# The opening of an eight-unit RWKV-7 recurrence, issued in another order

## The chip, the cores and the metric

The kernel runs on one core of one Trainium2 chip. The metric is the device time of one execution in microseconds, as the median of several runs. Engines are named as the profile names them: PE (TensorE matmul; PEld is its weight load), DVE (VectorE), ACT (ScalarE), POOL (GpSimd), SP (SyncE, which here issues DMAs only).

## The reference

The model is a two-layer decoder trunk over 1040 tokens (16 meta tokens and 1024 drawn ones). Layer 0 mixes tokens by an RWKV-7 recurrence, layer 1 by stick-breaking attention, and each layer has a conv-gated MLP. Only the recurrence bears on the change:

```python
def rwkv7_time_mix(x, ...):
    ...
    seq = tuple(jnp.moveaxis(t, 1, 0) for t in (rh, decay, kh, vh, -kk, kk * ah))
    def step(S, inp):
        r_t, w_t, k_t, v_t, a_t, b_t = inp
        sa = jnp.einsum('bhij,bhj->bhi', S, a_t)
        S = (S * w_t[:, :, None, :] + sa[..., None] * b_t[:, :, None, :]
             + v_t[..., None] * k_t[:, :, None, :])
        return S, jnp.einsum('bhij,bhj->bhi', S, r_t)
    S0 = jnp.zeros((bsz, N_HEADS, HEAD_DIM, HEAD_DIM), f32)
    _, y = lax.scan(step, S0, seq)
    ...                                  # group norm of y, bonus, gate g, output weight w_o
```

There are 16 heads of width 64; the state of a head is 64 x 64.

## The kernel before

The projections of layer 0 (up to 593 us in the trace) leave their results in DRAM scratch: `AR_s`, `BK_s`, `vc_s`, `g_s`, `b_s`. Then `rwkv_chain` runs the recurrence, and after it come the output weight, the MLP and layer 1.

**Tiling.** The recurrence is done by chunks of 64 tokens. A unit is (q, s): four of the 16 heads (two pairs, index u) and one of two halves of the sequence, with eight chunks (NC = 8). There are eight units, (0,0), (1,0), (2,0), (3,0), (0,1) and so on. The first 16 tokens are a chunk of their own, `first_chunk`, for all heads together. It gives the state that the four units of s = 0 start from.

**A unit is prepared by generators.** Each `yield` is a place at which another generator may be run:

- `stage_a` loads `BK` and `ARz` (2 and 4 DMAs, 2 MiB together), multiplies them into the blocks `Aa` (PE, masked copies by DVE), stores the diagonal 16 x 16 blocks to scratch (`AD`, 8 DMAs) and loads them back with one block in each partition (`AT`).
- `stage_s` inverts those blocks by 30 small dependent instructions (`substitute`; tiles `prd` and `XL`), on DVE for unit (0,0) and on POOL for the rest, and stores the result (`XD`).
- `stage_x` loads it back (`Dz`, 8 DMAs), and doubles the inverses from 16 to 32 and to 64 by three rounds of small matmuls: `g` and `x` (with DVE's transpose `DT`, ACT's copies `Gz` and `X`), then `G` (`GT`), then `G` again, into `XTb`.
- `stage_b`, `stage_t`, `stage_v` make `Ar`, `BKt`, `UV` and `KV`. `stage_f` is the group norm of the outputs.

`first_chunk` does the same in small: loads (`fa`, `fb`), products `A0`, blocks to scratch `AD0` and back as `AT0` (in `fb`), `substitute` on POOL (in `fg`), inverse to scratch `XD0` and back as `XT0` (in `fb`), then `c20`, `c30`, the states, `yp0`, and its own group norm.

**The chain.** `stage_c` does a unit's eight chunks one after another: c1 (state by `ARz`), `Rz` (DVE), c2 (`Rz` by `XTb`; halves `c` and `c2b`), copies to `UV` (DVE and ACT), c3, new state (DVE), and outputs `yp`. Between these it calls `gap()`, which runs pieces of the next units' generators by the strings in `SEQ`.

**What sets the order.** Before unit (0,0)'s chain the list `PRE` (L1413) sets the order of generator steps: a letter names a generator (a, b, s, t, v, x of unit (0,0); A and S of unit (1,0); p is `stage_a` of unit (2,0); f is `first_chunk`; c clears tiles; W warms PE with matmuls of no use), a number says how many steps. What is left is run afterwards, and `first_chunk` at least until its four states are there. PE's matmuls and all instructions that go through the wrapper `InOrder` (L36: `LQ` is SP, `V` is DVE, `G` is POOL) keep the order in which the program issues them. ACT's copies do not: a scheduler places them by its own estimate of when they are ready. Every engine executes its queue in order.

SP's DMAs signal eight semaphores in turn. A DMA that comes to a semaphore waits until the DMA eight places ahead of it, which signalled the same one, has landed.

## Time and profile before

| what | us |
|---|---|
| median of 3 runs | 3543.39 (3541.86 to 3548.19) |
| the profiled execution | 3554.61, of which 3551.8 is the span from first to last instruction |
| opening of the recurrence, last projection store to first c1 | 594.58 to 690.65 |
| the recurrence's eight units | 690.65 to about 1104 |
| PE busy over the span | 3126.4 (88%), 27421 instructions |
| DVE, ACT, POOL busy | 2277.8 (64%), 1546.3 (44%), 1617.6 (46%) |
| mean granted TensorE clock over the span | 0.936 |

Read it by stages: the shares are means over stages with different limits. In the opening, where the change is, no engine is busy for long, and the time goes to waits of one queue for another.

### The profile page before, as it was taken

The numbers are of one execution on the slowest core, as the hardware profiler recorded it, in microseconds if no ns is written. First come the engines' busy times: TensorE is split into PE (matmuls) and PEld (weight loads), VectorE is DVE, ScalarE is ACT, GpSimd is POOL, SyncE is SP. The second block draws the span as 40 slices with busy tenths as digits, with TensorE's granted clock in tenths as the row PEclk, the third lists the DMA queues.
The fourth block names the chain that finished last, engine by engine and source line by source line (L and its number), as shares of the span: only waits on it lengthen the run. The fifth ranks groups of instructions, "written<-read, shape, count | busy, mean of one in ns | idle before, by whom it ended". The sixth has DMA issues, their size and how long they took to land.

```text
span 3551.8 us, 66931 instructions
## 1 busy us (share of the span) xinstructions
PE 3126.4 (88%) x27421; PEld 2946.2 (83%) x27421; DVE 2277.8 (64%) x3047; ACT 1546.3 (44%) x2849; POOL 1617.6 (46%) x1469
## 2 busy tenths in 40 slices
PE   6997886588889799999899888888889699998998
PEld 5896665577778699999899888888788699998998
DVE  7779675133334888887542577777764988887342
ACT  4654542244443333333332366666654333334232
POOL 5556444222325554544321566666544544454221
PEclk8998998699988899999999899999999799999999
DMA  6344434233335222222654100101036122224453
GB/s 210 117 157 152 131 127 139 62 81 87 100 92 167 84 74 76 73 78 72 197 167 122 48 25 25 31 25 27 19 123 193 66 79 78 79 72 145 126 170 93
DMA packets 436716, 354.22 MB, mean 100 GB/s; under 512 B 66919, under 2 KB 360573, under 8 KB 436155
## 3 DMA queue, kind: packets, MB, share of 16 engines
q1 hardware_dynamic: 433883, 343.39, 31.8%
q0 software_dynamic: 2528, 6.57, 0.5%
q8 instruction: 215, 3.52, 0.4%
q14 instruction: 90, 0.74, 0.1%
HBM read 255.96 MB, written 93.92 MB: 99 GB/s over the span
## 4 chain that ended last, share of the span: by engine, by line
PE 47%; DVE 16%; ACT 6%; DMA 4%; issue 4%; POOL 3%; SPq 1%; ACTq 0%; DVEq 0%; POOLq 0%
PE dn L1577 12%; DVE t L1760 5%; DVE om L2314 2%; PE kps L2159 2%; DVE rs L1685 2%; PE c L826 2%; PE A L826 2%; PE wt L2162 2%; PE av L2159 1%; ACT t L1758 1%; PE vps L2159 1%; PE wo L1969 1%; POOL be L2317 1%; PE sop L2159 1%; PE z L2159 1%
## 5 line engine op out<-in xcount | busy, mean ns | idle before, releaser
L1577 PE MATMUL dn<-act,h_dn 128*128 128x260 f32 x2688 | 437.9, 284 | 6.2 <-ACT act L76 3.1
L1577 PEld LDWEIGHTS dn<-act,h_dn 128*128 128x128 f32 x2688 | 373.5, 190 | 7.5 <-ACT act L76 3.5
L1760 DVE SCALAR_TENSOR_TENSOR t<-u,pcol,t 128x1040 f32<-128x1040 f32 x168 | 304.2, 1811 | 108.6 <-ACT t L1758 108.5
L1577 PE MATMUL dn<-act,l_dn 128*128 128x260 f32 x1344 | 273.5, 285 | 1.8 <-POOL l_dn L1526 1.7
L2317 POOL TENSOR_TENSOR be<-be,om 128x911 f32<-128x911 f32 (+7 forms) x128 | 195.7, 1529 | 131.9 <-DVE om L2314 105.6
L1526 POOL TENSOR_TENSOR l_dn<-r_dn,h_dn 128x1024 fp32r<-128x1024 f32 (+1 forms) x46 | 102.9, 2237 | 326.0 <-ACT h_dn L76 325.5
L2314 DVE TENSOR_TENSOR_SCAN om<-om 128x912 f32<-128x912 f32 (+7 forms) x128 | 213.8, 1670 | 50.2 <-POOL om L2309 30.5
L76 ACT ACTIVATE h_dn<-r_dn 128x1024 fp32r<-128x1024 f32 (+1 forms) x92 | 90.7, 985 | 297.8 <-PE dn L1577 287.2
L1775 POOL TENSOR_TENSOR t<-t,t 128x1040 f32<-128x1040 f32 x42 | 103.3, 2460 | 250.6 <-DVE t L1760 250.6
L1577 PEld LDWEIGHTS dn<-act,l_dn 128*128 128x128 f32 x1344 | 207.4, 189 | 2.2 <-POOL l_dn L1526 2.2
L1526 POOL TENSOR_TENSOR s34l<-rs,s34h 128x1024 fp32r<-128x1024 f32 x44 | 106.1, 2410 | 101.9 <-ACT s34h L76 101.9
L76 ACT ACTIVATE WT<-wt 128x512 fp32r<-128x512 f32 (+2 forms) x224 | 98.7, 443 | 121.3 <-PE wt L2162 92.5
L2380 DVE TENSOR_TENSOR WT<-wt,WT 128x512 fp32r<-128x512 f32 (+2 forms) x224 | 107.7, 489 | 54.2 <-ACT WT L76 53.4
L2159 PE MATMUL av<-WT,VS 128*128 128x256 f32 (+3 forms) x640 | 108.9, 284 | 33.5 <-DVE WT L2380 33.4
L76 ACT ACTIVATE s34h<-rs 128x1024 fp32r<-128x1024 f32 x44 | 46.7, 1062 | 200.4 <-PE p001S L1712 4.9
L1526 DVE TENSOR_TENSOR l_dn<-r_dn,h_dn 128x1024 fp32r<-128x1024 f32 (+1 forms) x46 | 52.1, 1132 | 121.7 <-ACT h_dn L76 121.6
L2162 PE MATMUL wt<-ident,be 128*128 128x128 f32 x576 | 100.4, 298 | 33.6 <-DVE WTm L2355 33.5
L2159 PEld LDWEIGHTS av<-WT,VS 128*64 128x64 f32 (+1 forms) x640 | 85.9, 166 | 44.8 <-DVE WT L2380 43.7
L2309 POOL TENSOR_SCALAR_AFFINE_SELECT be<-be 128x128 f32<-128x128 f32 x128 | 78.9, 617 | 94.9 <-ACT be L2304 94.7
L44 POOL TENSOR_TENSOR prd<-AT,XL 128x15 f32<-128x15 f32 (+7 forms) x105 | 28.2, 269 | 204.8 <-DMA AT<-AD 197.1
L826 PE MATMUL A<-ARz,BK 128*128 128x128 f32 x512 | 94.2, 328 | 30.3 <-DMA ARz<-AR_s 19.3
L2162 PEld LDWEIGHTS wt<-ident,be 128*128 128x128 f32 x576 | 80.1, 155 | 39.5 <-DVE WTm L2355 36.2
(2142 smaller groups left out, 11035.6 us busy)
## 6 DMA issues: line engine op xcount, KB each, us to landing
r_dn<-in_ffn_down_dram SPq DMA_DIRECT2D x60, 512.0 KB
a_s<-t SPq DMA_DIRECT2D x84, 260.0 KB
rv<-in_ffn_up_dram SPq DMA_DIRECT2D x42, 512.0 KB
ra<-in_ffn_up_dram SPq DMA_DIRECT2D x42, 512.0 KB
araw<-a_s SPq DMA_DIRECT2D x50, 260.0 KB
r_dn<-in_ffn_down_dram SPq DMA_DIRECT2D x32, 384.0 KB
raw<-a_s SPq DMA_DIRECT2D x36, 260.0 KB
hr<-h_s SPq DMA_DIRECT2D x32, 260.0 KB
```

The costliest lines, as they stand in the source:

```text
L76: return S.activation(o, i, AF.Copy, scale=scale)
L826: return tc.keep_in_program_order(mm(*args, **kw))
L1526: eng.tensor_tensor(lo, x, f(hi), op=ALU.subtract)
L1577: self.mm(ps[:, c, :], w[:, kk, :], X[k][i][:, c * CH : (c + 1) * CH], start=k == 0 and j == 0, stop=k == len(X) - 1 and j == 2,)
L1760: VV.scalar_tensor_tensor(t[j], u[j][:, i : i + n], w, t[j], op0=ALU.mult, op1=ALU.add)
L1775: (G if n == L else VV).tensor_tensor(t[1], t[0], t[1], op=ALU.mult)
L2159: return tc.keep_in_program_order(mm(*args, **kw))
L2162: return tc.keep_in_program_order(nc.tensor.transpose(*args))
L2309: G.affine_select(out=t[0:nq, 0:nq], in_=t[0:nq, 0:nq], compare_op=ALU.is_ge, fill=fill, base=-nq, pattern=[[1, nq]], channel_multiplier=1,)
L2314: V.tensor_tensor_scan(om[0:nq, 0:nk], om[0:nq, 0:nk], om[0:nq, 0:nk], 1.0, op0=ALU.mult, op1=ALU.min)
L2317: G.tensor_tensor(be[0:nq, 1:nk], be[0:nq, 1:nk], om[0:nq, 0 : nk - 1], op=ALU.mult)
L2380: V.tensor_tensor(wt[:, 1, s0:s1], ps[:, s0:s1], f(wt[:, 0, s0:s1]), op=ALU.subtract)
```

## The change

Seven edits, all in the opening or in pieces that the opening and the units share:

1. `first_chunk` issues its four small loads `vc0` together with its `fa` loads.
2. It gets one more yield between the stores `AD0` and the load `AT0`.
3. Its product `kv0` comes ahead of its `substitute`.
4. Its stores `XD0` and loads `XT0` go by POOL's queue (`G`) where SP's (`LQ`) issued them.
5. `stage_a` gets one more yield between `AD` and `AT` for units (0,0) and (1,0), and `stage_s` of unit (0,0) stores `XD` by SP where POOL did.
6. In `stage_x` ACT's copy of the diagonal blocks into `X` is written behind the products `g` and their copy, where it stood ahead of them.
7. `PRE` is another list, and `needs` asks for less.

```diff
@@ first_chunk
-            yield
             for q in range(4):
                 qs = slice(2 * q, 2 * q + 2)
                 LQ.dma_start(vc0[:, qs], vc_s[0][q][:, :, 0:16])
+            yield
...
             for e in range(2):
                 LQ.dma_start(AD0[e].rearrange("p j t -> j p t"), Aa0[32 * e : 32 * e + 16, :, e, 0:16])
+            yield
...
             yield
+            ps = ps_t("kv0")
+            for p in range(NP):
+                for e in range(2):
+                    vs = slice(32 - 32 * e, 64 - 32 * e)
+                    pmm(ps[32 * e : 32 * e + 32, p * 64 : p * 64 + 64], Aa0[vs, p, e, :], UV0[vs, p, e, :], start=True, stop=True)
+            copy_act(fg[0:64, 0:512], ps[0:64])
+            yield
             G.tensor_copy(XL0, xinit0)
             yield from substitute(XL0, AT0, pr0, 16, lambda j: G, 4)
             G.memset(XT0, 0.0)
             XD0 = dr.tile([2, NP, 16, 16], F32, name="XD0")
             xdv = XD0.rearrange("e p (i g) t -> g (e p) i t", g=4)
             for g in range(4):
-                LQ.dma_start(xdv[g], XL0[32 * g : 32 * g + 16])
+                G.dma_start(xdv[g], XL0[32 * g : 32 * g + 16])
             for e in range(2):
-                LQ.dma_start(XT0[32 * e : 32 * e + 16, :, 0:16], XD0[e].rearrange("p j t -> j p t"))
-            yield
-            ps = ps_t("kv0")
...
+                G.dma_start(XT0[32 * e : 32 * e + 16, :, 0:16], XD0[e].rearrange("p j t -> j p t"))
@@ stage_a
+            if s == 0 and q < 2:
+                yield
             AT = ed["AT"] = place(f"AT{q % 2}", f"AT{nm}")
@@ stage_s
-            G.dma_start(XD.rearrange("b u c i t -> (b u c) (i t)"), XL.rearrange("p i t -> p (i t)"))
+            (G if s + q else LQ).dma_start(XD.rearrange("b u c i t -> (b u c) (i t)"), XL.rearrange("p i t -> p (i t)"))
@@ stage_x
-            copy_act(Xv[:, :, 0:16], D[:, :, 0:16])
             ps = ps_t(f"g16{nm}")
...
             copy_act(Gl[:, :, 0:16], ps[:, 0:256].rearrange("p (m t) -> p m t", t=16))
+            copy_act(Xv[:, :, 0:16], D[:, :, 0:16])
@@ rwkv_chain
         PRE = (
-            "a2 W2 f c2 a11 s9 A2 s9 f s9 b9 s9 f v t5 b11 A12 x2 f4 x3 f8 v20 x3 S10 f8 x3 S10 f8 x3 S12 "
-            "f20 x21 p2 W3 f "
+            "a2 f c A2 v a8 a f a f b9 A8 A A f s t5 f v20 s30 s x c f30 f x4 W2 f x4 f x6 p2 S33 W f "
         ).split()
...
-        needs = {"s": "a", "S": "A", "v": "a", "b": "a", "t": "a", "x": "cs"}
+        needs = {"s": "a", "S": "A", "x": "s"}
```

Behind `first_chunk`'s states, what is left of it (its group norm and its eight stores `y_s`) is no longer run in `PRE`: it is pulled by the gaps of unit (0,0).

On SP's queue, before: the last `fa` load, unit (0,0)'s eight stores `AD`, the load `AT`, and then unit (1,0)'s loads. A row's bracket says what it waits for; DMAHW0 to DMAHW7 are the eight semaphores in turn, and DVE, Pool and Activation are those engines.

```order
L44 DMA fa<-BK_s_124 128x2x64 [waits DMAHW0_49]
L44 DMA AD_5804<-Aa_5803 16x16x16 [waits DMAHW1_49,DVE_49]
L44 DMA AD_5804<-Aa_5803 16x16x16 [waits DMAHW2_49]
L44 DMA AD_5804<-Aa_5803 16x16x16 [waits DMAHW3_49]
L44 DMA AD_5804<-Aa_5803 16x16x16 [waits DMAHW4_49]
L44 DMA AD_5804<-Aa_5803 16x16x16 [waits DMAHW5_49]
L44 DMA AD_5804<-Aa_5803 16x16x16 [waits DMAHW6_49]
L44 DMA AD_5804<-Aa_5803 16x16x16 [waits DMAHW7_49]
L44 DMA AD_5804<-Aa_5803 16x16x16 [waits DMAHW0_49]
L44 DMA AT_5837<-AD_5804 128x256 [waits DMAHW4_49,DMAHW3_49,DMAHW5_49,DMAHW2_49,DMAHW6_49,DMAHW1_49,DMAHW7_49,DMAHW0_49,Pool_49]
L44 DMA BK_10_5850<-BK_s_122 128x1024 [waits Activation_49]
L44 DMA BK_10_5851<-BK_s_122 128x1024
```

And now, from the last of eleven loads that stand ahead of `AD` (four `vc0`, two `BK`, four `ARz`, one `vc`):

```order
L44 DMA vc_5807<-vc_s_129 128x2x512 [waits DMAHW3_49]
L44 DMA AD_5810<-Aa_5809 16x16x16 [waits DMAHW4_49,DVE_49]
L44 DMA AD_5810<-Aa_5809 16x16x16 [waits DMAHW5_49]
L44 DMA AD_5810<-Aa_5809 16x16x16 [waits DMAHW6_49]
L44 DMA AD_5810<-Aa_5809 16x16x16 [waits DMAHW7_49]
L44 DMA AD_5810<-Aa_5809 16x16x16 [waits DMAHW0_49]
L44 DMA AD_5810<-Aa_5809 16x16x16 [waits DMAHW1_49]
L44 DMA AD_5810<-Aa_5809 16x16x16 [waits DMAHW2_49]
L44 DMA AD_5810<-Aa_5809 16x16x16 [waits DMAHW3_49]
L44 DMA AD_5865<-fa 16x8x16 [waits DMAHW4_49,DVE_49]
L44 DMA AD_5865<-fa 16x8x16 [waits DMAHW5_49,DVE_49]
L44 DMA AT_5868<-AD_5810 128x256 [waits DMAHW3_49,DMAHW6_49,DMAHW2_49,DMAHW7_49,DMAHW1_49,DMAHW0_49]
```

The loads of unit (1,0) moved ahead of the stores, so that the eighth store stands eight places behind the load `vc` and shares its semaphore, DMAHW3; `first_chunk`'s two stores (`AD_5865`) moved ahead of `AT`.

On PE before, from the products of the first doubling to `first_chunk`'s c20 (`c_6416`); `kv_6398` is its kv0:

```order
L826 MATMUL g_6055<-DT_6045,Aa_5803 32x16 x64
L829 MATMUL vt_6131<-ident,vc_5974 64x128 x4
L829 MATMUL vt_6138<-ident,vc_5974 64x128 x4
L829 MATMUL vt_6145<-ident,vc_5974 64x128 x4
L829 MATMUL vt_6152<-ident,vc_5974 64x128 x4
L826 MATMUL kv_6159<-UV_6129,Aa_5803 64x64 x16
L826 MATMUL kv_6177<-UV_6129,Aa_5803 64x64 x16
L826 MATMUL x_6195<-Dz,Gz 32x16 x64
L826 MATMUL G_6286<-X32T_6047,Aa_5803 32x32 x32
L826 MATMUL G_6340<-XTb_5733,GT_6319 32x32 x32
L826 MATMUL kv_6398<-UV_5938,fa 32x64 x16
L826 MATMUL c_6416<-fg,fb 32x64 x16
```

And now, up to the first c1 of the chain (`c_6499`); each matmul here is two records in the trace:

```order
L826 MATMUL kv_6062<-UV_6014,Aa_5809 64x64 x16
L826 MATMUL g_6166<-DT_6162,Aa_5809 32x16 x64
L826 MATMUL warm<-ident 128x128 x4
L826 MATMUL c_6239<-fg,fb 32x64 x16
L826 MATMUL c_6258<-UV_5933,BKt_5932 64x64 x16
L826 MATMUL x_6275<-Dz,Gz 32x16 x64
L826 MATMUL G_6346<-X32T_6164,Aa_5809 32x32 x16
L826 MATMUL yp_6371<-fa,UV_5933 64x16 x16
L826 MATMUL G_6346<-X32T_6164,Aa_5809 32x32 x16
L826 MATMUL G_6408<-XTb_5733,GT_6405 32x32 x32
L826 MATMUL warm<-ident 128x128 x2
L826 MATMUL c_6499<-S_6363,ARz_5735 64x64 x4
```

`first_chunk`'s c20 and c30 moved from behind unit (0,0)'s doubling into it: they now stand between its products g and x.

On ACT before, from the start of unit (0,0)'s state (`PS000`) on; `X3210` is unit (1,0)'s X, `c2b000` the first c2:

```order
L76 ACTIVATE PS000_6532<-S00_6452,PC_160 128x64 x2
L76 ACTIVATE fb_5783<-yp0_6460 128x128
L920 ACTIVATE ysq0_6486<-fb_5783 128x128
L938 ACTIVATE g20_6493<-g00_6491 128x2
L76 ACTIVATE ysq0_6486<-g10_6492 128x128
L76 ACTIVATE BKt10_6543<-bt1000_6544 128x512
L76 ACTIVATE X3210_6681<-Dz_5766 128x16x16
L76 ACTIVATE UV00_6129<-c2b000_6554 64x2x64
```

And now:

```order
L1216 ACTIVATE XTb0_5733<-X3200_6163 32x16x32 x4
L76 ACTIVATE PS000_6498<-S00_6363,PC_160 128x64 x2
L76 ACTIVATE X3210_6662<-Dz_5766 128x16x16
L76 ACTIVATE fb_5777<-yp0_6371 128x128
L920 ACTIVATE ysq0_6509<-fb_5777 128x128
L76 ACTIVATE GT00_6405<-G00_6346 32x512 x2
L76 ACTIVATE XTb0_5733<-G200_6408 32x16x32 x2
L76 ACTIVATE BKt10_6512<-bt1000_6513 128x512
L76 ACTIVATE UV00_6014<-c2b000_6523 64x2x64
```

Unit (1,0)'s copy X, which waits for unit (1,0)'s `Dz`, moved from just ahead of the first c2's copy to ahead of unit (0,0)'s last two doublings (`GT00`, `XTb0`).

## Rows read from the trace of the kernel before

**Rows 1.** Busy time by windows, opening: window, length, engines, clock, DMA share, GB/s

```profile
594.58:690.65 96.07, 49.66 (x776) 43.88 (x776) 22.10 (x67) 18.26 (x39) 32.47 (x93) 0.65 0.34 73
```

**Rows 2.** Chain that ended last, 580 to 760: start us, us, what

```profile
652.55 1.88 DMA Dz<-XD
...
675.67 1.93 PE c L826 x32
...
678.87 1.97 PE c L826 x32
...
686.94 1.24 PE warm L826 x4
...
693.28 6.61 DMA ARz<-AR_s
```

**Rows 3.** Timeline of SP's issues: start us, us, queue, line, out<-in, count

```profile
607.60 0.52 SPq L44 DMA_DIRECT2D fa<-BK_s  x1
611.63 3.79 SPq L44 DMA_DIRECT2D AD<-Aa  x8
616.71 0.34 SPq L44 DMA_DIRECT2D AT<-AD  x1
...
628.07 0.69 SPq L44 DMA_DIRECT2D fb<-AD  x1
...
649.19 3.81 SPq L44 DMA_DIRECT2D Dz<-XD  x8
667.13 2.57 SPq L44 DMA_DIRECT2D XD<-fg  x4
...
694.68 7.00 SPq L44 DMA_DIRECT2D Dz<-XD  x8
```

**Rows 4.** Timeline of POOL; in brackets its idle time and what ended it

```profile
632.55 0.62 POOL L44 DMA_DIRECT2D XD<-XL  x1 [21.08 <-DVE XL L44]
...
634.39 0.21 POOL L44 TENSOR_TENSOR fg<-fb,fg 128x15 f32<-128x15 f32 x1
```

**Rows 5.** Timelines of DVE, PE and ACT, in order of time for each

```profile
618.86 0.17 DVE L44 TENSOR_TENSOR prd<-AT,XL 128x15 f32<-128x15 f32 x1 [7.25 <-DMA AT<-AD]
...
655.31 1.90 PE L826 MATMUL g<-DT,Aa 32*32 32x16 f32 x128 [12.38 <-DVE DT L44]
...
666.61 0.17 PE L826 MATMUL x<-Dz,Gz 32*32 32x16 f32 x1 [2.37 <-issue]
...
698.85 1.19 PE L826 MATMUL A<-ARz,BK 128*128 128x128 f32 x4 [7.50 <-DMA ARz<-AR_s]
...
700.83 0.37 PE L826 MATMUL c<-Rz,XTb 128*64 128x64 f32 x1
...
670.16 1.20 ACT L76 ACTIVATE GT<-G 32x512 f32<-32x512 f32 x2 [0.28 <-PE G L826]
673.36 1.18 ACT L76 ACTIVATE XTb<-G 32x512 f32<-32x512 f32 x2 [2.00 <-PE G L826]
...
702.99 0.42 ACT L76 ACTIVATE X<-Dz 128x256 f32<-128x256 f32 x1 [1.47 <-DMA Dz<-XD]
```

**Rows 6.** Windows: two of full DMA load, then three of substitutions (DVE, POOL, POOL)

```profile
600.00:605.00 5.00, 0.10 (x1) 0.13 (x1) 0.00 (x0) 0.00 (x0) 4.85 (x4) 0.50 1.05 200
620.00:625.00 5.00, 1.26 (x6) 1.29 (x7) 4.52 (x20) 0.00 (x0) 0.00 (x0) 0.50 1.03 300
...
618.86:622.70 3.84, 0.00 (x0) 0.00 (x0) 3.31 (x16) 0.00 (x0) 0.00 (x0) 0.50 0.98 344
634.39:637.78 3.39, 2.68 (x15) 1.94 (x16) 0.00 (x0) 3.05 (x7) 2.53 (x12) 0.85 0.02 5
728.24:738.95 10.71, 10.16 (x241) 8.50 (x236) 3.97 (x14) 7.57 (x20) 8.18 (x30) 1.00 0.24 76
```

**Rows 7.** DMA issues, 630 to 745: count, KB each, median us to landing

```profile
XD<-XL POOLq DMA_DIRECT2D x3, 128.0 KB, 2.0
```

**Rows 8.** Tile stA on POOL: count, ns min/median/max of one

```profile
L1599 POOL TENSOR_TENSOR stA<-stA x24: 1287/1313/2300, 1114.3 to 2753.7; 128x520 f32<-128x520 f32 x24
```

More of the change, by code (lines that the diff above doesn't have):

```diff
@@ L1042, in first_chunk @@
             for g in range(4):
-                LQ.dma_start(xdv[g], XL0[32 * g : 32 * g + 16])
+                G.dma_start(xdv[g], XL0[32 * g : 32 * g + 16])
             for e in range(2):
-                LQ.dma_start(XT0[32 * e : 32 * e + 16, :, 0:16], XD0[e].rearrange("p j t -> j p t"))
-            yield
-            ps = ps_t("kv0")
-            for p in range(NP):
-                for e in range(2):
-                    vs = slice(32 - 32 * e, 64 - 32 * e)
-                    pmm(ps[32 * e : 32 * e + 32, p * 64 : p * 64 + 64], Aa0[vs, p, e, :], UV0[vs, p, e, :], start=True, stop=True)
-            copy_act(fg[0:64, 0:512], ps[0:64])
+                G.dma_start(XT0[32 * e : 32 * e + 16, :, 0:16], XD0[e].rearrange("p j t -> j p t"))
             yield
```

## Prediction, made before the changed kernel ran

> **What bounds the kernel now.** I read the windows first: the opening lasts 96.07 us, and in it PE is busy for 49.66, POOL for 32.47, DVE for 22.10, DMA for a third [rows 1]. No engine is the limit there, so what it costs is set by one queue waiting for another. The chain of waits and the queues say which. Unit (0,0)'s inverse is ready when POOL stores it at 632.55 [rows 4], and lands 2.0 us later [rows 7], but SP issues the loads `Dz` only at 649.19 [rows 3]: ahead of them on SP stand unit (1,0)'s stores `AD`, which wait for PE. That is 14 us of queue order. First_chunk's inverse starts at 634.39 [rows 4], is interleaved with unit (1,0)'s on POOL, and is stored only at 667.13 [rows 3]; c20 follows at 675.67, c30 at 678.87 [rows 2]. Last, unit (2,0)'s loads are issued behind first_chunk's output stores, so PE stands 7.50 us before A at 698.85, and c2 of the first chunk, which PE has behind A, starts at 700.83 [rows 2, 5]. From there the eight units run as a chain. I measure the change at that c2.
>
> **The change, part by part.**
>
> *Loads ahead of the stores (edits 1, 2, 5, 7).* The last `fa` load is issued at 607.60, taking 0.52 [rows 3]. Four `vc0` loads at 0.64 each (the pace of the four `XD` in 2.57, rows 3) end at 610.7. Then come 2.62 MB: `BK`, `ARz` and `vc`. By the ring of eight, the eighth store `AD` waits for `vc` to land. At 300 GB/s that is 8.7 us, at 200 it is 13.1, the two paces of full queues [rows 6]; with 2.0 for a landing [rows 7], 621.4 or 625.8. I take 621.4, since the 300 is from this same set of loads. Before, `AT` was issued 1.8 after the last of the eight stores (616.71 against 614.95, the eighth at a pitch of 0.47 in the 3.79) and the substitution began 2.15 after that, at 618.86 [rows 3, 5]. So `AT` is issued at 623.2 and DVE starts at 625.4, 6.5 later than before. This is the price of the change; what it buys comes now.
>
> *Unit (0,0)'s inverse.* DVE's 30 instructions go at 0.24 each (16 in 3.84, rows 6), 7.2 us, since the masked copies that interrupted them now stand ahead of them: 632.6. The store goes by SP, whose queue then has only unit (1,0)'s `AD` and `AT` ahead, done by about 631. It lands at 634.6. From the first `Dz` load to g was 6.12 (649.19 to 655.31, rows 3, 5), so g starts at 640.7 instead of 655.31, ends 1.90 later [rows 5], and eight warm records take 2.5 (1.24 for four, rows 2): PE is free for c20 at 645.1.
>
> *First_chunk's inverse by POOL's queue.* Its blocks are stored with unit (0,0)'s, last at 622.6, and loaded back from about 624.3. The landing is between 2.15, as for `AT`, and 6.3, the 628.07 to 634.39 of before [rows 3, 4], in which POOL was itself busy until 634.3; I take 2.15, since the transfers have one size: 626.5. POOL's 30 instructions go at 0.28 each (12 in 3.39, rows 6): 635.0. They now run beside DVE's substitution. No row shows the two side by side. The bound below is nothing; above, POOL waits for each of DVE's, 30 at 0.21 (3.31 us for 16, rows 6), 6.2. The `stA` instructions, many of them beside DVE's, have a median of 1313 ns over a minimum of 1287 and a maximum of 2300 [rows 8], so I take a quarter, 1.5: 636.5. Clearing and four stores at 0.62 [rows 4] end at 639.3, land at 640.7; two loads end at 641.9 and land at 643.3. SP's queue no longer carries these, and POOL's waits once for a landing, with unit (1,0)'s substitution behind it. c20 starts at 645.1, when PE comes to it: 1.8 of slack.
>
> *The doubling behind c20 and c30.* c20 to c30 was 3.20 and c30 takes 1.97 [rows 2], x about 1.9, like g: x ends at 652.2. Before, from x's end (666.78) to `GT` was 3.4 [rows 5]; first_chunk's yp0 between the halves of G adds under 2. `GT` could start at 657.5.
>
> *What is late next.* ACT has unit (1,0)'s X ahead of `GT`. That X waits for unit (1,0)'s substitution: POOL comes free for it at 641.9, copies 0.4, runs 30 instructions in 10.7 [rows 6], 653.0, stores, 655.0. `Dz` takes 5.2 from first issue to landing (649.19 to 654.43, rows 2, 3): 660.2. X (0.42, rows 5) and two copies of first_chunk's outputs, under 0.7, put `GT` at 661.3. Its 1.20, and 3.18 from its end to the end of `XTb` (671.36 to 674.54, rows 5), make 665.7; on PE warm, c1, A and bt, the last two 1.98 long (698.85 to 700.83, rows 5), stand ahead of c2. Unit (2,0)'s A no longer waits: its loads go out behind the first `Dz`, near 639. c2 starts near **668**, 32.8 earlier.
>
> *In the units.* X no longer holds up the first c2's copy (1.47 of waiting at 702.99, rows 5). Against it stand first_chunk's norm, two PE products, eight small DVE and four ACT instructions, some of them in PE's and DVE's waits; I bound them between 0 and 3 us and take 1.2. In units (1,0) and (2,0) ACT's order moves by a place or two at X; within 1.5 either way, taken as nothing. The eight `y_s` stores now stand on SP behind unit (2,0)'s `AT`, ahead of loads needed a unit later: nothing. Behind the opening every engine's order is otherwise the same up to a few rows in layer 1, so the shift should reach the end.
>
> *Sum.* 32.8 + 1.5 - 1.2, about 33 us. The profiled execution took 3554.6, 0.3% over the median of 3543.4: it would become 3521.5, and the median **3510**.
>
> **The rivals.**
>
> *Most of the burst is paid, 3523.* The loads come at 200 GB/s (4.4 later), the broadcast load takes its 6.3 (4.1), POOL and DVE alternate (4.7). All lie on POOL's one chain to `GT`, so they add: with one and a half of three, some 7 to 8 us, with all 13, a gain of 20 and 3523; of less if POOL's small transfers land later than 2.0. For it: each is a row. Against: the three have separate causes. On the port between DVE and POOL the rows decide only that some of POOL's instructions take longer. The Trainium skill, SBUF — State Buffer, section "Who interferes with whom", goes further: a DVE instruction with two SBUF inputs and a GpSimd one that reads SBUF exclude each other, and the second waits for the first to end. By that rule alone the 4.7 are due in full and the time is 3515; the maximum of rows 8 agrees with it, the median doesn't tell.
>
> *The stall moves, no change, 3543.* The shift is swallowed behind the opening: some wait in the recurrence that goes by a queue not fed by the chain. Against: from 700.83 on the loads of each unit are issued when the one before frees its tiles, so they shift along.
>
> *Slower: POOL's chain.* Place: POOL from first_chunk's blocks to unit (1,0)'s `Dz`, 626.5 to 660.2, 33.7 us long in my sum, with ACT's X behind it and `GT`, so c2, behind X. It is one queue with two landings inside, and every microsecond more of it goes into c2 after the first 3 (for X). It decides for slower when it is twice as long, 33 us more; 45 more give 3555. That takes POOL's DMAs of 64-byte rows at some 7 us each, six of them, where the stores of 1 KB rows took 0.62 to issue and 2.0 to land [rows 4, 7]. No row shows POOL issuing such small rows, SP's took 0.64 [rows 3].
>
> *It gains more, 3500.* The slack terms all fall well, and PE's clock, granted at 0.65 on average in the opening [rows 1], rises to its higher level earlier in the first unit.
>
> **How the numbers follow.** Forecast (a gain of 26 to 40 us, 3503 to 3517): 0.64. Burst paid (gain of 8 to 26, 3517 to 3535): 0.21. No change: 0.06. Slower: 0.05. More than 40: 0.04. Faster by over 0.2% (7 us, about what a measurement of this kernel can tell from no change): 0.64 + 0.21 + 0.04 = 0.89. Within 0.2%: 0.06; slower: 0.05. The range goes from 3501, where the forecast's favourable ends lie (no contention, 1.5, the norm for nothing, 1.2, a clock or a queue better by 6), to 3527, where the sum of the burst's three prices and a few microseconds for POOL's small transfers lies; it leaves out some 0.18.
>
> **What would show it right or wrong.** Right: `AD` on SP stretched from 3.8 to about 7 us, with its eighth near 621; DVE's 30 instructions unbroken from 625; `Dz` of unit (0,0) near 635; first_chunk's `XD` on POOL near 637; ACT's longest wait of the opening before unit (1,0)'s X near 660, and c2 near 668. Wrong: `AD` still done by 616 or later than 627; POOL's `fg` instructions over 0.4 us apart; PE waiting for c20's operands instead of being late for them; a wait of more than 3 us for a load in unit (0,0); or a recurrence that ends less than 25 us earlier although c2 came 33 us earlier.

## The result, and the profile after

The changed kernel took 3518.1 us as the median of four runs (3509.4 to 3521.6) beside 3545.8 for the kernel before: a ratio of 0.9919, 95% interval 0.9898 to 0.9940. In a second comparison it was 3515.1 (six runs) beside 3550.2, 0.9913 (0.9891 to 0.9936). The forecast was 3510 with a range of 3501 to 3527, a ratio of 0.9906: faster, as forecast, and in the range. The profiled execution was the fastest of its four, 3509.4 (span 3507.1); the profiled one of before, 3554.6, lay above every time of its own kernel in this comparison. So the two traces are 44.7 us apart, the medians 28 and 35, and a part of what follows is about the difference.

Busy time by windows of the changed kernel, from the first load `BK` to the first c1 (columns as in [rows 1]):

```profile
593.16:666.40 73.24, 45.33 (x772) 40.31 (x772) 22.05 (x60) 17.96 (x38) 34.65 (x96) 0.69 0.58 133
```

The stretch of [rows 1] is 22.8 us shorter with about the same work in it. What went are waits: the DMA share rose from 0.34 to 0.58. SP's issues now (timeline as in [rows 3]):

```profile
606.59 3.49 SPq L44 DMA_DIRECT2D fb<-vc_s  x4
...
614.54 7.41 SPq L44 DMA_DIRECT2D AD<-Aa  x8
...
623.70 0.34 SPq L44 DMA_DIRECT2D AT<-AD  x1
624.13 0.68 SPq L44 DMA_DIRECT2D fb<-AD  x1
...
634.73 0.34 SPq L44 DMA_DIRECT2D XD<-XL  x1
636.46 4.09 SPq L44 DMA_DIRECT2D Dz<-XD  x8
640.66 0.86 SPq L44 DMA_DIRECT2D BK<-BK_s  x2
...
655.73 4.36 SPq L44 DMA_DIRECT2D Dz<-XD  x8
```

The eight stores `AD` take 7.41 where [rows 3] had 3.79, behind the 2.62 MB that now stand ahead of them. Counted from the first load `BK`, DVE's substitution starts after 33.4 us (at 626.57) instead of 24.3 (618.86 in [rows 5]): the price is 9.1. Unit (0,0)'s `Dz` goes out at 636.46 instead of 649.19. POOL, as in [rows 4]:

```profile
627.26 0.22 POOL L44 TENSOR_TENSOR fg<-fb,fg 128x15 f32<-128x15 f32 x1 [16.07 <-DMA fb<-AD]
...
636.43 2.09 POOL L44 DMA_DIRECT2D XD<-fg  x4
640.42 1.09 POOL L44 DMA_DIRECT2D fb<-XD  x2 [1.90 <-DMA XD<-fg]
641.51 0.41 POOL L44 COPY XL<-xinit 128x256 f32<-128x256 f32 x1
...
652.77 0.61 POOL L44 DMA_DIRECT2D XD<-XL  x1 [0.30 <-POOL XL L44]
```

First_chunk's inverse leaves at 636.43 instead of 667.13, POOL waits 1.90 for its landing, and unit (1,0)'s substitution follows. PE, then ACT, up to the first c2 (as in [rows 5]):

```profile
642.86 1.91 PE L826 MATMUL g<-DT,Aa 32*32 32x16 f32 x128 [6.06 <-DVE DT L44]
...
647.13 1.92 PE L826 MATMUL c<-fg,fb 32*32 32x64 f32 x32
...
662.80 0.31 PE L826 MATMUL G<-XTb,GT 32*32 32x32 f32 x2 [3.37 <-ACT GT L76]
...
667.03 1.22 PE L826 MATMUL A<-ARz,BK 128*128 128x128 f32 x4
...
668.88 0.27 PE L826 MATMUL c<-Rz,XTb 128*64 128x64 f32 x1
...
661.07 0.42 ACT L76 ACTIVATE X<-Dz 128x256 f32<-128x256 f32 x1 [3.13 <-DMA Dz<-XD]
...
662.16 1.20 ACT L76 ACTIVATE GT<-G 32x512 f32<-32x512 f32 x2
```

A no longer waits for `ARz` (7.50 in [rows 5]). The late wait is now the one that the forecast named: ACT's X of unit (1,0) stands 3.13 us before `Dz`, `GT` behind it, and PE 3.37 before `GT`. c2 starts at 668.88 instead of 700.83.

From c2 to the next unit's first c1 it takes 39.25 us where it took 43.56. This stretch as one window, of before and then of after (columns as above):

```profile
700.83:744.39 43.56, 39.28 (x865) 33.00 (x864) 16.81 (x49) 20.66 (x56) 8.76 (x31) 0.91 0.23 60
```

```profile
668.88:708.13 39.25, 36.68 (x869) 31.20 (x869) 17.86 (x56) 20.49 (x57) 9.60 (x33) 1.00 0.21 55
```

PE is busy for 2.6 us less with about the same records; the granted clock, 0.91 on average before and 1.00 after (0.50 and 1.00 are 1.2 and 2.4 GHz), goes with that. Two waits of PE in the kernel before, which the changed kernel does not have there, make 0.78 and 0.77 more:

```profile
703.76 0.58 PE L826 MATMUL c<-UV,BKt 128*64 128x64 f32 x5 [0.78 <-ACT UV L76]
...
724.34 0.63 PE L829 MATMUL vt<-ident,vc 128*64 128x128 f32 x4 [0.77 <-issue]
```

The first is what ACT's X, waiting for `Dz` ahead of the copy `UV`, cost; the second ends without anything that the profile shows. Windows of the clock, of before and then of after:

```profile
704.00:708.00 4.00, 4.00 (x40) 3.10 (x38) 1.05 (x4) 1.74 (x5) 0.00 (x0) 0.50 0.18 65
708.00:712.00 4.00, 4.00 (x57) 3.55 (x57) 1.80 (x6) 1.73 (x5) 0.00 (x0) 0.94 0.01 4
```

```profile
664.00:668.00 4.00, 4.00 (x64) 3.59 (x61) 0.58 (x2) 1.18 (x2) 0.00 (x0) 0.50 0.02 4
668.00:672.00 4.00, 4.00 (x57) 3.28 (x56) 0.82 (x4) 2.50 (x8) 0.00 (x0) 0.92 0.00 0
```

Before, the clock was still at the lower level up to 708, over 7 us behind the first c2; after, it rises with the first c2.

### The profile page after: what moved, and what is told of

It reads as the page before. It is cut to its first block, busy times and chain, and to the rows that moved or that the text cites. A ratio compares the mean times of both kernels' runs of the same rounds, so it can differ in the third digit from the quotient of the medians.

```text
span 3507.1 us, 66917 instructions
## 1 busy us (share of the span) xinstructions
PE 3103.8 (89%) x27413; PEld 2923.3 (83%) x27413; DVE 2278.0 (65%) x3047; ACT 1546.7 (44%) x2849; POOL 1621.1 (46%) x1474
## 5 line engine op out<-in xcount | busy, mean ns | idle before, releaser
L1528 POOL TENSOR_TENSOR s34l<-rs,s34h 128x1024 fp32r<-128x1024 f32 x44 | 106.1, 2411 | 102.3 <-ACT s34h L76 102.3
L2164 PEld LDWEIGHTS wt<-ident,be 128*128 128x128 f32 x576 | 79.5, 154 | 39.3 <-DVE WTm L2357 36.2
L2306 ACT ACTIVATE be<-z 128x346 f32<-128x346 f32 (+5 forms) x224 | 99.8, 446 | 24.5 <-PE z L2161 24.0
L44 DVE TENSOR_TENSOR Rz<-c,KV 64x128 f32<-64x128 f32 x128 | 36.9, 289 | 108.9 <-PE c L826 94.7
```

What stands on the lines that cost most here:

```text
L1528: eng.tensor_tensor(lo, x, f(hi), op=ALU.subtract)
L2164: return tc.keep_in_program_order(nc.tensor.transpose(*args))
L2306: S.activation(be[0:nq, c : c + w], ps[0:nq, 0:w], AF.Sigmoid, scale=0.125)
```

## The experiments

All numbers below come from one profile of each kernel; the medians of several runs stand in the last column. "Load to c2" is from the first `BK` load of unit (0,0) to the first c2, so that the start of the recurrence, which differs by up to 4 us from one profile to the next, doesn't enter. Two cautions for reading it. The changed kernel itself has two profiles (after and after_again), and their first columns differ by 1.6 us. And the medians of the changed kernel and its variants, 3515 to 3528, have intervals of some 9 us either way: they tell these kernels from the kernel before, but not from one another. What is said below of differences among the variants rests on one profile each.

| kernel | load to c2 | c2 to next c1 | from there to the end | median us |
|---|---|---|---|---|
| before | 106.2 | 43.6 | 2807.4 | 3546 to 3551 |
| old_order | 102.3 | 43.5 | 2813.0 | 3547.0 |
| p2_early | 97.4 | 40.8 | 2815.3 | 3542.9 |
| after | 75.7 | 39.3 | 2798.9 | 3518.1 |
| after_again | 77.3 | 39.4 | 2797.5 | 3515.1 |
| xd0_by_sp | 77.8 | 41.3 | 2815.3 | 3528.0 |
| xd00_by_pool | 84.5 | 41.8 | 2814.2 | 3521.0 |
| x10_by_pool | 75.9 | 39.3 | 2820.1 | 3522.9 |
| xt0_by_sp | 74.4 | 39.2 | 2814.9 | 3517.1 |
| dz10_early_x10 | 74.4 | 39.8 | 2807.0 | 3519.0 |
| own_first_x10 | 69.4 | 41.0 | 2819.2 | 3521.2 |
| own_first_nw | 67.7 | 43.7 | 2816.7 | 3519.9 |
| warm_in_wait | 78.0 | 39.6 | 2809.9 | 3523.7 |
| warm_fill | 75.9 | 40.5 | 2800.1 | 3522.0 |

### Which part carries the gain

**old_order** keeps edits 3, 4, 6 and the SP store of edit 5, and takes back the list, the yields and `needs` (the list is shown):

```diff
-            "a2 f c A2 v a8 a f a f b9 A8 A A f s t5 f v20 s30 s x c f30 f x4 W2 f x4 f x6 p2 S33 W f "
+            "a2 W2 f c2 a11 s9 A2 s9 f s9 b9 s9 f v t5 b11 A12 x2 f4 x3 f8 v20 x3 S10 f8 x3 S10 f8 x3 S12 "
+            "f20 x21 p2 W3 f "
```

> The list PRE, needs and the three yields of before, with the other edits kept: kv0 early, XD0 and XT0 by POOL's queue, unit (0,0)'s XD by SP's, X copied behind the products. Theory: the gain is the order, the other edits only let it be: Dz of unit (0,0) is still issued near 649 behind unit (1,0)'s AD, POOL still interleaves the two substitutions until 667, unit (2,0)'s ARz still come behind first_chunk's y_s; c20 comes 0 to 2 earlier than 675.67, c2 at 698 to 701 (700.83 before), the total within 4 us of before. Rival: the queues (POOL's for XD0, SP's for XD) carry the gain: c2 under 690, a total of 3520 to 3535.

```profile
693.33 1.19 PE L826 MATMUL A<-ARz,BK 128*128 128x128 f32 x4 [8.38 <-DMA ARz<-AR_s]
```

The row of PE's timeline shows the wait for `ARz` still there (8.38). c2 is 4 us better than before by the table, not 0 to 2; the total is the same (ratio 0.9991, 0.9974 to 1.0008, so a gain of up to 9 us is not excluded). The queue edits alone carry at most a small part of the gain.

**xd00_by_pool** takes back the second half of edit 5 in the changed kernel: `G.dma_start(XD...)` for every unit.

> Unit (0,0)'s inverse is stored by POOL again (edit 5's second half undone), so that first_chunk's instructions stand behind that store in POOL's queue, and it waits for DVE's substitution, which ended at 634.65. ACT's order now has unit (1,0)'s X behind GT. Theory (a queue's order sets the opening, DVE's and POOL's substitutions must run side by side): fg starts near 635.3 instead of 627.26, XT0 is issued near 648.5, c20 starts at 651 instead of 647.13; unit (1,0)'s substitution starts near 650, its X would come near 669 but now stands behind GT, so c2 follows c20: near 672 to 673, 3 to 4 later. DVE's 30 instructions, alone, take 7.2 instead of 8.1. If the X stood in front as before, c2 would be near 677. Rival: POOL had slack of 8 us, c2 within 1 of 668.88.

POOL's timeline, then PE's:

```profile
635.14 0.62 POOL L44 DMA_DIRECT2D XD<-XL  x1 [25.35 <-DVE XL L44]
...
646.94 2.06 POOL L44 DMA_DIRECT2D XD<-fg  x4
655.60 1.08 POOL L44 DMA_DIRECT2D fb<-XD  x2 [6.60 <-DMA XD<-fg]
...
657.58 2.38 PE L826 MATMUL c<-fg,fb 32*32 32x64 f32 x32 [8.83 <-DMA fb<-XD]
```

The direction is the theory's, c2 8.8 later by the table where 3 to 4 were expected. The rest is the 6.60, where the changed kernel waited 1.90: `XD0`'s four stores of 4 KB now go out beside unit (2,0)'s 2 MiB of loads. The median, 3521.0, does not show the loss.

**xd0_by_sp** takes back edit 4: `LQ.dma_start` for `XD0` and `XT0`.

> first_chunk's stores XD0 and loads XT0 go back to SP's queue (edit 4 undone), where they stand behind unit (0,0)'s Dz loads; all else as changed. In the changed kernel SP is done with Dz at 640.55 and c2 of the first chunk comes at 668.88. Theory: c2 hangs on POOL's one chain, and in it POOL waits 1.90 for the landing of XD0 and spends 3.2 on issuing; without these, unit (1,0)'s substitution starts near 637 instead of 642.0, its Dz lands near 656 and ACT's X no longer holds up GT. XD0 is then stored at 640.6 to 643.1, XT0 issued near 645 and landed near 648, so c20 starts near 648.5 instead of 647.13 and becomes the late one: GT near 661 instead of 662.16, c2 near 667.5, 1 to 1.5 earlier. Rival: c2 hangs on PE's own path, so that POOL's queue is what bought c20: c2 later by the 1.4 to 4 by which c20 is later. Total time: within 3 us of the changed kernel by either.

It came out 2.1 later than in the changed kernel's first profile and 0.5 later than in its second, so the table doesn't decide whether it lost. The rival's cause is not there: c20 was late by 0.40 of waiting only. Unit (1,0)'s substitution did start early (POOL's copy `XL` at 637.21), but SP came to its `Dz` late, behind first_chunk's g and b loads, so ACT's X waited even longer (SP's, then ACT's timeline):

```profile
657.98 5.11 SPq L44 DMA_DIRECT2D Dz<-XD  x8
...
664.17 0.42 ACT L76 ACTIVATE X<-Dz 128x256 f32<-128x256 f32 x1 [5.20 <-DMA Dz<-XD]
```

**p2_early** is the kernel before with one item moved:

```diff
-            "f20 x21 p2 W3 f "
+            "p2 f20 x21 W3 f "
```

> The kernel before with one item of PRE moved: unit (2,0)'s loads (p2) ahead of first_chunk's last steps, where they stood behind its output stores. It has none of the change's edits. Theory: PE's 7.50 us of waiting for ARz before A is a wait of queue order alone, so it goes: A follows c1 near 691.5, c2 near 693.5 (700.83); ACT's order puts unit (1,0)'s X behind the second c2's copy, so nothing takes the place; with PE no longer idle the clock rises earlier than 708, and the next unit's c1 comes 8 to 11 earlier than 744.39. Total 8 to 11 us under before. Rival: another wait takes its place (unit (1,0)'s Dz or X, first_chunk's norm), c2 earlier by less than 4.

PE's timeline:

```profile
690.17 1.22 PE L826 MATMUL A<-ARz,BK 128*128 128x128 f32 x4
...
692.18 0.37 PE L826 MATMUL c<-Rz,XTb 128*64 128x64 f32 x1
```

A follows c1 without a wait: c2 8.8 earlier, the next c1 11.5 earlier in terms of the table's two columns, as the theory had it. Of the 8.8 the wait is 7.5; the other 1.3 came ahead of c1, where the edit changes little. Of the 2.7 behind c2, 0.78 is PE's wait for `UV`, which goes because ACT's X now stands behind the second c2's copy, and 2.0 is PE's shorter busy time. The ratio, 0.9983 (0.9965 to 1.0002), fits 7 us and does not prove it. So of the changed kernel's 30 us up to c2 some 7.5 are this one wait. That the rest needs the two inverses early and together is argued from the rows: no run has one of them without the other.

Edit 6 has no run of its own. In old_order, which keeps it, ACT has X between the same two copies as in the kernel before (`BKt`, X, `UV`), so there it moved nothing; its share in the changed kernel is not shown. Edits 1 to 3 were not taken back one by one.

### The late wait behind the change

**x10_by_pool**:

```diff
-            copy_act(Xv[:, :, 0:16], D[:, :, 0:16])
+            (G.tensor_copy if (q, s) == (1, 0) else copy_act)(Xv[:, :, 0:16], D[:, :, 0:16])
```

> Unit (1,0)'s copy of the diagonal blocks into X is made by POOL where ACT made it ahead of GT; every other engine's order is the same. Theory: that copy, waiting 3.13 us for unit (1,0)'s Dz at 661.07, is the late wait of the opening, so without it GT starts when G and the two copies of first_chunk's outputs are done, at 659.4 to 660.2 instead of 662.16, and c2 at 666.2 to 667.0 instead of 668.88: 2 to 2.7 earlier. Rival: GT is late for another reason (G's own end at 659.43, ACT's copies), c2 moves by less than 1. The end of the recurrence moves by as much as c2; the total by less than a run's scatter.

POOL's, PE's and ACT's timeline:

```profile
643.45 1.08 POOL L44 DMA_DIRECT2D fb<-XD  x2 [4.02 <-DMA XD<-fg]
...
649.72 2.33 PE L826 MATMUL c<-fg,fb 32*32 32x64 f32 x32 [4.39 <-DMA fb<-XD]
...
662.47 1.20 ACT L76 ACTIVATE GT<-G 32x512 f32<-32x512 f32 x2 [0.37 <-PE G L826]
```

c2 didn't move (75.9 against 75.7). `GT` now follows G directly, so X was in its way; but c20 was 2.6 late, since `XD0` landed 2 us later in this execution. The one hid the other.

**xt0_by_sp** moves only the two loads `XT0` to SP:

```diff
-                G.dma_start(XT0[32 * e : 32 * e + 16, :, 0:16], XD0[e].rearrange("p j t -> j p t"))
+                LQ.dma_start(XT0[32 * e : 32 * e + 16, :, 0:16], XD0[e].rearrange("p j t -> j p t"))
```

> first_chunk's stores XD0 stay on POOL's queue, but its two loads XT0 go by SP, where they stand behind unit (0,0)'s Dz and ahead of unit (2,0)'s 2 MiB of loads. In the changed kernel POOL waited 1.90 for XD0's landing, with unit (1,0)'s substitution behind; with two other kernels that wait was 4.02 and 6.60, where the stores went out beside unit (2,0)'s loads. Theory (a small transfer's landing is set by the burst it meets, and POOL's wait is paid by unit (1,0)): XD0 now lands ahead of that burst, so XT0 is issued on SP within 1 us of the end of Dz; POOL's substitution of unit (1,0) starts 0.5 after its XD0 issues instead of 3.5; its X comes near 659 (661.07) and c2 at 666.5 to 667.5 (668.88), c20 unchanged within 0.5. Rival: SP's queue is the tighter one; first_chunk's g and b loads, pushed behind, hold up unit (1,0)'s Dz as they did where XD0 went by SP too (Dz at 657.98), X at 661 or later, c2 at 669 or later.

POOL's, SP's and ACT's timeline:

```profile
638.50 0.44 POOL L44 COPY XL<-xinit 128x256 f32<-128x256 f32 x1
...
639.98 0.78 SPq L44 DMA_DIRECT2D fb<-XD  x2
...
659.17 0.41 ACT L76 ACTIVATE X<-Dz 128x256 f32<-128x256 f32 x1 [2.10 <-DMA Dz<-XD]
```

POOL goes on 3 us earlier, X comes at 659.17 and c2 at 667.14, as expected. **dz10_early_x10** adds unit (1,0)'s `Dz` ahead of the g and b loads (one more step of its `stage_x` in `PRE`) and X by POOL.

> The same with two things more: unit (1,0)'s Dz loads are issued ahead of first_chunk's eight g and b loads, and its X is copied by POOL. Theory: no engine on the path to GT then has a foreign wait ahead of it; c20 at 647 or earlier, GT directly behind G and two ACT copies, 0.4 to 0.8 after G's end near 659.4, c2 at 666 to 667, 2 to 3 earlier than 668.88 and 0 to 1 earlier than with XT0 by SP alone; unit (1,0) is ready near 658. Rival: c20 comes late for a DMA of its own (XT0), then c2 follows c20 by 21.7, as 647.13 to 668.88, less the 2.7 of X.

c2 came at 669.68, 74.4 after the first load, no better than xt0_by_sp. `GT` stood directly behind G again (0.37), but c20 came at 650.56: unit (0,0)'s `Dz` could go out only 3.58 after the issue of its `XD`, where the changed kernel needed 1.73. From that store's issue to the first `Dz` load it took 1.7 to 2.1 in five of the traces, 3.6 to 3.8 in three whose queues differ little from theirs, without a cause that they show, and 4.1 and 4.5 beside the loads of own_first_x10 and own_first_nw. Differences of 1 or 2 us in c2 are therefore not settled by one profile, and by medians these two are no faster than the changed kernel.

### The price of the burst

**own_first_x10** is dz10_early_x10 with `XT0` back on POOL and with the loads in another place (the list against the changed kernel's; the step `y` at its end is dz10_early_x10's):

```diff
-            "a2 f c A2 v a8 a f a f b9 A8 A A f s t5 f v20 s30 s x c f30 f x4 W2 f x4 f x6 p2 S33 W f "
+            "a2 f c a8 a f a f v A2 b9 f s t5 f v20 s30 s x A8 A A c f30 f x4 W2 f x4 f x6 p2 S33 y W "
```

> Unit (1,0)'s loads, the load vc and unit (1,0)'s products stand behind unit (0,0)'s and first_chunk's stores and loads AD, AT and behind unit (0,0)'s transposes, where the changed kernel has them ahead; also unit (1,0)'s X by POOL and its Dz ahead of the g and b loads. This prices the burst (6.5 us in the prediction, AD stretched from 3.8 to 7.4). Theory: AD takes 3.8 again, AT is issued near 617, DVE's substitution starts at 619 to 620 instead of 626.57 and POOL's fg likewise (627.26), g near 637 behind unit (1,0)'s products (their loads land near 630), c20 641 to 643, c2 660.5 to 663, 6 to 8 earlier than 668.88. Rival: the burst is only moved: it now meets XD0, XT0 or Dz, or PE stands before unit (1,0)'s products, and c2 stays at 666 or later.

SP's timeline:

```profile
607.74 3.93 SPq L44 DMA_DIRECT2D AD<-Aa  x8
```

`AD` takes 3.93 again, DVE's substitution starts at 615.17, which is 9 us earlier counted from the first load (the forecast had paid 6.5), and c2 comes 6.3 earlier by the table than in the changed kernel, 5.0 earlier than in dz10_early_x10. That c2 gains less than the 9 has one reason in the trace: PE stands 2.56 in the middle of G, for nothing that the profile shows. **own_first_nw** also drops the eight warm records between g and c20 (`W2`).

> Unit (0,0)'s and first_chunk's blocks ahead of unit (1,0)'s loads, as in the run before (c2 at 660.41), and without the eight warm records (2.50 us) between g and c20. Theory: c20 then follows g, since its operands were there in time; c2 2 to 2.5 earlier, near 658, ten us ahead of the changed kernel; the clock's level of 0.50 in that stretch does not depend on the warm records. Over the whole, 3505 to 3515, by 5 to 12 us faster than the changed kernel on the same chip, if the scatter lets it be seen. Rival: XT0 is late for c20 by itself (it was issued at 631.99 to 633.08), c2 stays at 660; or without them PE's clock rises later and the first unit gives it back.

c2 is 8 us ahead of the changed kernel's, but the next c1 only 3.6, and the total, 3519.9, is no better. DVE, then PE:

```profile
661.17 0.71 DVE L44 STREAM_TRANSPOSE DT<-Dz 128x512 f32<-128x512 f32 x1 [3.83 <-DMA Dz<-XD]
661.92 0.28 DVE L44 COPY UV<-c 64x128 f32<-64x128 f32 x1
...
662.25 0.45 PE L826 MATMUL c<-UV,BKt 128*64 128x64 f32 x8 [2.11 <-DVE UV L44]
```

The stall has moved to the next unit: the transpose of unit (1,0)'s `Dz` stands on DVE ahead of the first c2's copy, and that unit's loads are now the late ones. PE waits 2.11 in the middle of the chunk, and the clock, 1.00 from 660 to 662, is back at 0.50 from 664 to 668. So at least a part of the price that unit (0,0) pays for the burst is paid for unit (1,0).

### The clock

**warm_in_wait** and **warm_fill** both add eight warm records (`W2`); in the first they fell behind the second G, in the second ahead of it, in PE's wait.

> PE's wait of 3.37 us between G and the second G, for GT, is filled with eight warm matmul records (2.50 us at the lower clock level); otherwise the changed kernel. In it the granted clock is 0.50 from 644 to 668 and 1.00 from about 668 on, 5 us after PE's wait ended; in the kernel before, it rose near 708, 8 us after PE's wait of 7.50 ended. Theory (the extra 4 us of the first unit, 39.3 from c2 to the next unit's first c1 instead of 43.6, come from the clock, which rises once PE has no long wait any more): the clock reaches 1.00 up to 3 us earlier, c1, A and bt take less, c2 up to 1.5 earlier at the same GT, or the stretch from c2 to the next unit's c1 up to 1 shorter. Rival: the clock rises by something else than PE's idleness: same rise near 668, c2 from 0 to 0.3 later.

> As the run before was meant: eight warm records now stand between G and the second G, in PE's wait of 3.37 us for GT (in that run they fell behind the second G, where PE did not wait, and c2 came 1.65 later). Theory (the rise of the clock follows PE's last long wait): PE is then without a wait of over 1 us from 655 on, the clock reaches 1.00 by 665 to 666 instead of 668.3, c1, A and bt take 1 to 1.5 less, c2 comes 1 to 1.5 earlier at the same GT. Rival: the rise does not come earlier, c2 within 0.3 of the changed kernel at the same GT; then what PE does in those 3 us does not set it.

In warm_in_wait c2 came 2.3 later by the table than in the changed kernel's first profile. PE's row shows why: behind the second G stand 12 warm records where the changed kernel has four of 1.22 us, and nothing covers the difference of 2.56:

```profile
664.34 3.78 PE L826 MATMUL warm<-ident 128*128 128x128 f32 x12
```

In warm_fill PE's wait for `GT` shrank to 1.28 (PE's timeline):

```profile
663.00 0.31 PE L826 MATMUL G<-XTb,GT 32*32 32x32 f32 x2 [1.28 <-ACT GT L76]
```

Its windows (columns as above):

```profile
664.00:668.00 4.00, 4.00 (x71) 3.59 (x68) 0.58 (x2) 1.17 (x2) 0.00 (x0) 0.50 0.02 4
668.00:672.00 4.00, 4.00 (x46) 3.32 (x44) 0.58 (x3) 1.47 (x3) 0.00 (x0) 0.64 0.00 0
```

The clock rose no earlier (0.64 from 668 to 672, where the changed kernel had 0.92), so the forecast of a rise by 665 to 666 failed. It is one profile, and the same program rises at different moments: in the changed kernel's second profile, where PE's wait for `GT` ended at 666.01, the level was still 0.50 up to 672:

```profile
668.00:672.00 4.00, 4.00 (x40) 3.51 (x34) 0.58 (x2) 1.17 (x2) 0.00 (x0) 0.50 0.02 4
```

What sets the moment stays open. What stands is the rows: the lower level up to 708 before and up to about c2 after, and some 2 us of PE's busy time gone with p2_early's wait.

### The same kernel again

> The changed kernel once more, with more rounds and a second profile. Theory (the change ends with unit (0,0); behind it the traces differ by the granted clock alone, which falls for 4 to 10 us in other places in each execution): c2 of the first chunk again within 2 us of 668.88, from c2 to the next unit's c1 39.2 to 39.8 (43.6 before), but from there to the end 2807 to 2820 as in the other traces, where the first profile had 2799 and the kernel before 2807; the gain by medians 30 to 36 us. Rival: the changed order also shortens the later units, 2797 to 2802 again, a gain of 40 or more.

c2 came at 672.25, 3.4 later than in the first profile where 2 were allowed; 1.8 of it is a later start. `GT` waited for X again (3.49 on ACT), and c20 now waited too (PE's timeline):

```profile
649.63 2.27 PE L826 MATMUL c<-fg,fb 32*32 32x64 f32 x32 [1.55 <-POOL XL L44]
```

The rest to the end was 2797.5, as the rival said and not 2807 to 2820. But the rival's gain of 40 and more isn't there: the medians differ by 35 and 28. Both profiles of this kernel lie under the median of its runs, that of before above its own, and the kernels whose order behind unit (0,0) is nearly the same spread from 2800 (warm_fill) to 2820 (x10_by_pool). If what a profile lies off its median is taken off the third column, that column becomes 2799 to 2804 for before and 2801 to 2808 for the changed kernel (an estimate from the table and the medians): no gain there. What the units of the recurrence differ by is mostly the clock. Durations of units 1 to 6 (c1 to c1), and the granted clock in each:

| kernel | 1 | 2 | 3 | 4 | 5 | 6 |
|---|---|---|---|---|---|---|
| before | 51.1 / 0.97 | 54.4 / 0.91 | 51.3 / 0.97 | 50.7 / 0.97 | 54.4 / 0.87 | 47.7 / 0.89 |
| after | 50.6 / 0.97 | 51.2 / 0.97 | 51.6 / 0.97 | 51.1 / 0.97 | 51.2 / 0.97 | 47.8 / 0.86 |
| after_again | 50.5 / 0.97 | 52.1 / 0.93 | 51.0 / 0.97 | 55.9 / 0.88 | 50.5 / 0.93 | 44.3 / 1.00 |
| xt0_by_sp | 50.8 / 0.97 | 51.4 / 0.97 | 54.7 / 0.91 | 56.7 / 0.85 | 54.2 / 0.81 | 46.4 / 0.89 |

Two windows behind it, unit 5 of before and the same unit of after:

```profile
951.94:1006.33 54.39, 47.51 (x916) 41.11 (x913) 19.88 (x59) 23.04 (x61) 14.90 (x37) 0.87 0.27 70
```

```profile
912.64:963.82 51.18, 43.40 (x917) 37.24 (x913) 19.78 (x59) 23.06 (x61) 14.96 (x37) 0.97 0.28 75
```

The same instructions, the same DVE and ACT time; PE is busy 4.1 us longer and the unit takes 3.2 longer. Units of this kind turn up in most of the kernels, at another place each time; among the first five units of after and of warm_fill, two of the three lowest in the table's third column, there is none. Where it begins is seen in unit 4 of after and after_again, the same program. PE waits there for ACT's copy `UV` in both profiles (3.25 and 3.93), and the windows behind that wait are, of after:

```profile
873.00:877.00 4.00, 3.31 (x30) 3.13 (x30) 0.98 (x5) 1.48 (x5) 0.00 (x0) 0.57 0.32 121
877.00:881.00 4.00, 3.07 (x34) 2.56 (x32) 2.61 (x6) 0.27 (x1) 0.00 (x0) 1.00 0.00 0
```

and of after_again:

```profile
877.00:881.00 4.00, 2.80 (x28) 2.68 (x29) 0.98 (x5) 1.55 (x5) 0.00 (x0) 0.56 0.49 135
881.00:885.00 4.00, 4.00 (x30) 3.37 (x30) 1.27 (x3) 0.16 (x1) 0.00 (x0) 0.58 0.00 0
```

In both the clock falls; in the second it stays down about twice as long, and it falls once more from about 895 to 901; the first stays at 1.00 (51.1 against 55.9 us). So I read the 10 us between the traces behind unit (0,0) as this scatter, not as the change; that a small part of it is the change's can't be excluded.

## Why the prediction was right, point by point

- **What bounds the kernel.** Right: queues waiting for one another. Queue edits without the order give 4 us at c2 and nothing that the total shows (old_order); one wait taken from the old order alone is worth its 7.5 at c2 (p2_early); the order with one queue taken back loses 9 (xd00_by_pool), with the other 2 or nothing (xd0_by_sp).
- **Loads ahead of the stores.** Right and a little low. `vc0` ended at 610.1 (610.7), the eighth `AD` went out at 621.65 (621.4), `AT` at 623.70 (623.2), DVE started at 626.57 (625.4). As the trace of after began 1.4 earlier, DVE was 2.6 late by the forecast's own count: the price is 9, not 6.5, from before to after and again by own_first_x10. The `vc0` loads and the landings of `vc` and `AT` each took a little longer than their terms.
- **Unit (0,0)'s inverse.** g at 642.86 instead of 640.7. Beside the later start, DVE's 30 instructions took 8.1 us, not 7.2; alone, in xd00_by_pool, they took 7.2.
- **First_chunk's inverse, and the port.** `fg` started at 627.26 (626.5): the broadcast landed within 3.1, nearer to 2.15 than to 6.3. The step that was wrong is who pays for the overlap: I charged POOL 1.5, but its 30 instructions took 8.9 beside DVE's and 8.8 alone in xd00_by_pool, so it is DVE that lost, the 0.9. The Trainium skill, SBUF — State Buffer, "Who interferes with whom", has the second of the two wait for the other's whole instruction; by that rule alone the time would have been 3515. The rows show contention, but 1.0 us of it in all where the wait of one queue for each instruction of the other was put at 6.2.
- **POOL's own DMAs.** Issue 0.52 each (0.62 taken), POOL's wait 1.90 (1.4). The Trainium skill, DMA: Bandwidth & Descriptors, "Anatomy of one DMA — SWDGE (gpsimd) path", gives some 2.0 us for a small transfer. The median from issue to landing was 1.7 here, which agrees, but 6.8 in xd00_by_pool beside 2 MiB of loads, which doesn't. So the rival "slower" had its mechanism, and was spared by the moment at which the stores go out. That is in part luck: with the same order up to there POOL waited 2.17 in after_again and 4.02 in x10_by_pool. Nor could the 1.8 of slack for c20 be relied on: PE came to it without a wait in the first profile, but waited 1.55 in after_again and 4.39 in x10_by_pool, which is a sign that the forecast had named for being wrong.
- **What is late next.** Right in name and size: ACT's X at 661.07 (660.2), `GT` at 662.16 (661.3), c2 at 668.88 (668). The trace of after began 1.4 earlier, so by the table the gain to c2 is 30.5 and in the second profile 29.0, not 32.8: the lateness above, 2 to 4 us in all.
- **In the units.** Wrong in the terms, and on the good side: I had +1.5 for X and -1.2 for the norm, and it was 4.3 from c2 to the next c1. X was worth 0.78, the norm cost nothing that shows, another 0.77 is a wait of PE without a cause in the profile, and most of it, 2.6, goes with the clock, which stood only in a rival.
- **Sum.** 30.5 and 4.3 are 34.8, in the second profile 29.0 and 4.1, 33.1; the sum said 33. Two errors of 2 to 4 us cancelled; that the sum came out this close is luck, though each step of the path is the one forecast. The medians' 28 and 35 lie around it. The forecast of 3510 is 5 to 8 under the measured medians although the gain was right, because it hung on the 3543.4 of three runs, and the kernel before took 3546 to 3551 in the later comparisons.

The rival "gains more" (3500) showed in the difference of the two profiles alone, not in the medians. "The stall moves" did not happen here; it did in own_first_nw.

## What to carry to other kernels

Where no engine is busy, write down each queue in order and ask for each row which landing it waits for and who stands behind it; then the new order can be summed row by row, and it came out within 4 us of 33. When such a chain is shortened, look at once for the next one: the load burst that was put ahead for unit (1,0) costs unit (0,0) 9 us, and when it was taken away, own_first_nw had given back more than half of its 8 us at c2 by the next unit's c1. An effect of 2 us isn't decided by one profile when small transfers land after 2 to 7 us and the clock falls at another place in each execution: take marks near the change, counted from a common start, and take totals from medians.

## What the hardware showed unexpectedly

- With a PE wait of 3 to 4 us the clock fell to 0.50 and came back after about 3.5 us in one execution and 7 in another of the same program. Units 1 to 5 of the table last from 50.5 us at 0.97 to 56.7 at 0.85. The Trainium skill, TensorE: Matmul & The Clock Gate, Part 1: The HAM clock gate, says that the rise comes at another point from run to run of one kernel; these traces agree.
- More PE work ahead of the chunk did not bring the rise forward in the one profile taken: with PE's wait of 3.37 cut to 1.28 it came near 671, against 668 to 669 and, in the second profile of the changed kernel, between 672 and 673.
- A 4 KB store by POOL's queue landed after 1.7 us beside unit (0,0)'s `Dz` loads (after) and after 6.8 us beside a 2 MiB burst on SP's queue (xd00_by_pool), each the median of four stores in one profile.
- With 30 small instructions on DVE beside 30 on POOL, DVE's took 8.1 us where they took 7.2 alone, POOL's 8.9 where they took 8.8 (after, xd00_by_pool).
